# A streaming-encoder block: the mixer's values as one wide block, and its scaled queries in tiles of their own

## The chip, the cores and the metric

One core of a Trainium2 chip runs the whole program. The metric is the device time of one execution in microseconds (us), and the number of a kernel is the median of its runs. For explaining, one execution is recorded by the hardware profiler; its span runs from the first to the last instruction.

The engines are TensorE (PE: matrix products into PSUM; PEld is its loading of weights), VectorE (DVE), ScalarE (ACT), GpSimd (POOL) and SyncE (SP, which issues the DMAs here). Each takes its instructions in order; semaphores make one wait for another.

## What is computed

256 frames of 2048 features go through one layer: a feed-forward half-step, a mixer, an attention over 256 memory tokens, a second feed-forward half-step. All is float32. The change lies in the mixer. Cut to what matters, with its four heads and chunks of 64 frames:

```python
h = rms_norm(x, mix_norm)
u, q, k, v, g, a_lr = split(h @ w_in)          # 1024, 512, 512, 1024, 1024, 16 columns
y_pool = pool_mixer(u, pool_w, pool_scale)     # 4 groups: trailing means - token, then a 256x256 map
# gated linear attention, per head (dk 128, dv 256), chunk-causal:
log_a  = log_sigmoid(a_lr @ w_a2 + b_a) / 16;  cum = cumsum(log_a) in the chunk
k_dec  = k * exp(b_end - cum)                  # b_end: cum at the end of the chunk
scores = q_scaled . k_dec                      # q_scaled has the decay of the chunks between
o      = scores @ v;  o = rms_norm(o) * head_norm * silu(g)
x = x + concat(y_pool, o) @ w_out
```

## The kernel before, in words

**Units of weights.** All large products are made of units of one MB of weights (128 x 2048 floats in SBUF). A unit is loaded by SP into `raw` (three buffers), split into a rounded high part (`wh`, ACT) and a rest (`wl`, DVE), three buffers each, and then used by PE: high by high, high by rest, rest by high, three products for each 128-row step and half of the frames. `Stream.emit` writes the program out: ahead of a unit's products it puts the split of the unit two further on, and behind each split the load of the unit three further on. `st.op(f, n)` puts a piece of work behind the n-th unit from there. The chain `in_turn` keeps the splits in order on ACT and DVE; all the rest may be set between by the framework's planner, which fixes each engine's order at compile time by its own estimate of the times. So an engine's order need not be that of the program.

**Three forms of a block.** `block_a` (weights stationary, the frames streaming) gives the result transposed and holds two PSUM tiles `pa`. `block_b` (frames stationary) makes 512 columns out of four units of 24 products and holds one PSUM tile `pb`. `block_s` (`block_t` without sevens is its plain form) makes 1024 columns out of eight units. For a pair of 128-row steps for which sums of the frames' blocks were computed ahead (`Sums`, here `qk_sums` for the pairs 1 and 3, kept in `ys` 12 to 15), its unit is a "seven": seven block products in place of eight, 21 instructions in place of 24. A seven's weights are summed first on DVE (`T`, L486), and then two sets are split: `xh`, `xl` (one buffer each in the mixer) and `wh`, `wl`. Its PSUM is two tiles for whole results from the first unit on and two more for parts from the first seven on; behind the last seven `combine` adds up the parts (L574 to L579), and behind the last unit `join` adds both (L589).

**PSUM** has four tiles of two banks each (`ptile`), for everything.

**The mixer's order.** First queries and keys (one `block_s` of 1024 columns, with `qk_sums`), then the decay (`load_a`, `decay`), then the pool's columns (two `block_a`, groups 0 and 1, then 2 and 3), the values (two `block_b` of 512 columns, written to `v` by `ev_v`, L1137), with the pool's own product (`pool_unit`, L1027) between these two, then the gate (two `block_a`), then `w_out`. Around the values:
- `ev_pool` (L986) turns a pool group's product into its means: a chain of DVE steps (L319, L323, L997, L1001, L1005) in three `m4` tiles, of which there are three in all, and a split into `ys` 8 + 2g.
- `scores(h)` (L1142) copies and scales the queries (L1150 on ACT, L1152 on DVE) into another `m4` tile, multiplies with the keys (L1160, PSUM tile `pq`) and copies the result to `ST` (L1166). The four stand behind 0, 2, 4 and 6 units counted from the start of the values.
- `pool_out(g)` scales and splits the pool's product from PSUM (`pp`) into `ys` 2g and 2g + 1 (L236 on ACT, L240 on DVE).
- `attend(h)` (L1168) multiplies scores and values (PSUM tile `po`) and squares and copies the result (L1182 on ACT, L1184 on DVE); `head_norms` and `head_scale` normalise the heads, `ev_g` applies the gate.

Of the kernel before, what the change touches and what calls it, by code (L numbers as in the profile page):

```python
# [7 lines left out]
F32 = mybir.dt.float32  # L8
F32R = mybir.dt.float32r
AF = mybir.ActivationFunctionType  # L10
# [12 lines left out]
H = 4  # L23
# [76 lines left out]
def build(ctx, tc, I, out):  # L100
# [187 lines left out]
    def split_pair(dst, kt, src):  # L288
        split(dst[:, kt : kt + 2, 0, :], dst[:, kt : kt + 2, 1, :], src)
# [315 lines left out]
    def block_b(srcs, act, evict, delay=0):  # L605

        n_k = 4 * len(srcs)
        held = {}

        def unit(gi):  # L610
            def fn(wh, wl):
                if gi == 0:
                    held["ps"] = ptile(uid("pb"))
                wh, wl = (w.rearrange("p (k n) -> p k n", n=NB) for w in (wh, wl))
                for kk in range(4):
                    k = 4 * gi + kk
                    for h in range(2):
                        products(held["ps"][:, h, :], act, k, h, wh[:, kk], wl[:, kk],
                                 k == 0, k == n_k - 1)
            return fn  # L620

        for gi, src in enumerate(srcs):
            st.unit(src, unit(gi))
        st.op(lambda: evict(held["ps"]), delay)
# [6 lines left out]
    def wblock(w, n0, k0=0, nk=KT):  # L631

        def src(k):
            return lambda raw: wload(raw.rearrange("p (k n) -> p k n", n=NB), w, k, 4, n0)
        return [src(k0 + k) for k in range(0, nk, 4)]
# [311 lines left out]
    ffn(I["ffn1_w_gate"][0], I["ffn1_w_up"][0], I["ffn1_w_down"][0], down_first,  # L947
        amid_first)
    st.op(close_scope, 1)
    MIX_HOMES = {"T": [("v", D, 1)], "xh": [("xh", 3 * NB, 1)], "xl": [("xl", 3 * NB, 1)]}  # L950
    st.op(open_scope("s_mix", MIX_HOMES), 1)


# [3 lines left out]
    def mt(name, shape, tag=None, bufs=1):  # L957
        t = whole_lines(scope["pool"], shape, F32, tag or name, uid(name), bufs)
        mix[name] = t
        return t  # L960

    def mixer_constants():
        keep = mt("keep", [P, S])
        nc.gpsimd.memset(keep, 1.0)
        for c in range(S // CH):
            nc.gpsimd.memset(keep[:, c * CH : c * CH + 1], 0.0)
        wa2 = mt("wa2", [32, H * DK])
        for i in range(2):
            nc.sync.dma_start(wa2[16 * i : 16 * i + 16, :], I["gla_w_a2"][0])
        for h in range(H):  # L970
            s = mix["ST", h] = mt("ST", [P, 2, S], bufs=H)
            nc.gpsimd.memset(s[64:128, 0, 0:CH], 0.0)
            nc.gpsimd.memset(s[64:128, 1, 2 * CH : 3 * CH], 0.0)

    st.op(mixer_constants, 2)

    def m4():
        return scope["pool"].tile([P, 2 * 2 * (S + PAD)], F32, tag="m4", name=uid("m4"), bufs=3)
# [3 lines left out]

    def as_four(t):
        return t[:, : 4 * S].rearrange("p (a b) -> p a b", a=4)

    def ev_pool(b):  # L986
        def evict(p, ps):
            g = 2 * b + p
            w = WINDOWS[g]
            u, s0, s1 = (as_pad(m4()) for _ in range(3))  # L990
            L = S + PAD
            nc.gpsimd.memset(u[:, :, :PAD], 0.0)
            joined(ps, u[:, :, PAD:], rows["R"])
            src, dst, other, n = u, s0, s1, 1
            while n < w:
                lo = 2 * n - 1
                nc.vector.tensor_tensor(  # L997
                    out=dst[:, :, lo:L], in0=src[:, :, lo:L], in1=src[:, :, lo - n : L - n], op=ALU.add
                )
                src, dst, other, n = dst, other, dst, 2 * n  # L1000
            nc.vector.scalar_tensor_tensor(  # L1001
                out=src[:, :, PAD : PAD + w - 1], in0=src[:, :, PAD : PAD + w - 1], scalar=float(w),
                in1=bc(invc[:, : w - 1]), op0=ALU.mult, op1=ALU.mult,
            )
            nc.vector.scalar_tensor_tensor(  # L1005
                out=src[:, :, PAD:], in0=src[:, :, PAD:], scalar=1.0 / w, in1=u[:, :, PAD:],
                op0=ALU.mult, op1=ALU.subtract,
            )
            split_pair(ys, 8 + 2 * g, src[:, :, PAD:])
        return evict  # L1010

    def load_pool(raw):
# [5 lines left out]
    def pool_unit(wh, wl):  # L1018
        wh, wl = (w.rearrange("p (g t d) -> p g t d", g=4, t=2) for w in (wh, wl))
        for g in range(4):  # L1020
            if g % 2 == 0:
                two = ptile(uid("pp"))
            ps = two[:, g % 2, :].rearrange("p (a b) -> p a b", a=2)
            for dt in range(2):
                parts = [(w, ct, a) for ct in range(2) for w, a in ((wh, 0), (wl, 0), (wh, 1))]
                for n, (w, ct, a) in enumerate(parts):
                    nc.tensor.matmul(  # L1027
                        ps[:, dt, :], w[:, g, ct, dt * P : (dt + 1) * P],
                        ys[:, 8 + 2 * g + ct, a, :], start=n == 0, stop=n == 5,
                    )  # L1030
            mix["pp", g] = ps

    def pool_out(g):
        for dt in range(2):
            split_scaled(ys, 2 * g + dt, mix["pp", g][:, dt, :], gcol(G_PS + 2 * g + dt))
# [93 lines left out]
    block_a(wblock(w_in, 0), xs, ev_pool(0))  # L1129
    block_a(wblock(w_in, NB), xs, ev_pool(1))  # L1130

    def ev_v(b):
        def evict(ps):
            if b == 0:
                mt("v", [P, 2, 2 * NB])
            for h in range(2):
                nc.scalar.activation(  # L1137
                    mix["v"][:, h, b * NB : (b + 1) * NB], ps[:, h, :], AF.Copy, scale=Rcol[:, h : h + 1]
                )
        return evict  # L1140

    def scores(h):  # L1142
        q, kd, E, F = mix["q"][:, h, :], mix["k"][:, h, :], mix["E"], mix["F"]
        e = lambda c: E[:, 4 * h + c : 4 * h + c + 1]
        f = lambda i: F[:, i, h : h + 1]
        QD = m4()
        at = (0, 3 * CH, 5 * CH)
        factors = {(0, 1): e(1), (0, 2): f(0), (0, 3): f(2), (1, 2): e(2), (1, 3): f(1), (2, 3): e(3)}
        for j in range(3):
            nc.scalar.copy(QD[:, at[j] + j * CH : at[j] + (j + 1) * CH], q[:, j * CH : (j + 1) * CH])  # L1150
            for c in range(j + 1, 4):
                nc.vector.tensor_scalar_mul(  # L1152
                    QD[:, at[j] + c * CH : at[j] + (c + 1) * CH], q[:, c * CH : (c + 1) * CH],
                    factors[j, c],
                )
        ps = ptile(uid("pq"))
        for j in range(4):
            part = slice((j % 2) * CH, (j % 2 + 1) * CH)
            rhs = QD[:, at[j] + j * CH : at[j] + S] if j < 3 else q[:, 3 * CH :]
            nc.tensor.matmul(  # L1160
                ps[part, j // 2, j * CH : S], kd[:, j * CH : (j + 1) * CH], rhs, start=True, stop=True
            )
        s = mix["ST", h]
        for j in range(4):
            part = slice((j % 2) * CH, (j % 2 + 1) * CH)
            nc.vector.tensor_copy(s[part, j // 2, j * CH :], ps[part, j // 2, j * CH : S])  # L1166

    def attend(h):  # L1168
        s, v = mix["ST", h], mix["v"]
        po = ptile(uid("po"))  # L1170
        for vt in range(2):
            col = h * DV + vt * P
            nc.tensor.matmul(  # L1173
                po[:, vt, :S], v[:, 0, col : col + P], s[:, 0, :], start=True, stop=False
            )
            nc.tensor.matmul(
                po[:, vt, 2 * CH : S], v[:, 1, col : col + P], s[:, 1, 2 * CH :], start=False, stop=True
            )
        if h % 2 == 0:
            mix["oz", h // 2] = as_four(m4())  # L1180
        q = mix["osq", h] = ttile()
        nc.scalar.activation(q, po[:, :, :S], AF.Square)  # L1182
        i = h % 2
        nc.vector.tensor_copy(mix["oz", h // 2][:, 2 * i : 2 * i + 2, :], po[:, :, :S])  # L1184
# [37 lines left out]
            split_pair(ys, 8 + 2 * h, t)  # L1222
        return evict

    for h, after in enumerate((0, 2, 4, 6)):
        st.op(lambda h=h: scores(h), after)
    for b in range(2):
        block_b(wblock(w_in, (4 + b) * NB), xs, ev_v(b))
        if b == 0:
            st.unit(load_pool, pool_unit)  # L1230
            for g in range(4):
                st.op(lambda g=g: pool_out(g))
        for i in range(2):
            h = 2 * b + i
            at = 1 + i - b
            st.op(lambda h=h: attend(h), at + 1)
            st.op(lambda h=h: head_squares(h), at + 1)
        st.op(lambda b=b: head_norms(b), 5 - 2 * b)
        st.op(lambda b=b: head_scale(b), 6 - b)
    block_a(wblock(w_in, 6 * NB), xs, ev_g(0), (0, 0))  # L1240
    block_a(wblock(w_in, 7 * NB), xs, ev_g(1))
    st.op(close_scope, 1)
# [401 lines left out]
```

## Time and profile before

| what | value |
|---|---|
| median of 3 runs | 2090.24 us (2089.54 to 2092.51) |
| profiled execution, its own time | 2089.89 us |
| its span, first to last instruction | 2088.1 us |
| DMA moved | 435.94 MB, mean 209 GB/s |
| values products L362 `pb` | 192 (128 + 64), 0.39 us each by themselves |
| stage of the values, 812 to 871 us | PE busy 59.00 us, DVE 38.23, ACT 23.40 |

How to read it: the page gives busy time by engine, the span in 40 slices, the DMA queues, the chain of work that ended last, and the costliest groups of instructions by line. Products of PE overlap, so the time from one to the next is less than the duration of one. In a list of waits a row says who waited for whom, for how long in all, how often, and the longest. In a table of windows a row has the window, its length, busy time and number of instructions of PE, PEld, DVE, ACT and POOL, the granted clock of PE, the DMA share and GB/s. In the chain and the timeline a row begins with its start and its length in us.

### The profile page before, as it was taken

Reading aid. Unit: us, or ns where it says so; the run is one execution under the profiler, and the core shown is the slowest. Engines: PE = TensorE matmul, PEld = TensorE weight load, DVE = VectorE, ACT = ScalarE, POOL = GpSimd, SP = SyncE. Lnnn points to the kernel's source line nnn. Section 1 sums busy time; section 2 is a strip of 40 time slices with the busy share of each in tenths; the row PEclk is TensorE's granted clock in tenths of the full one; section 3 lists DMA queues with packets and bytes.
Section 4 is the critical chain, followed back from the end, with each engine's and each line's share of the span. In section 5 each row is a group of like instructions: output and inputs, shape, how many; then the busy total and the mean of one; then the engine's idle time right before and its main releaser. Section 6 shows DMA issues by size and latency. Waiting matters only on the chain.

```text
span 2088.1 us, 24282 instructions
## 1 busy us (share of the span) xinstructions
PE 2069.6 (99%) x9591; PEld 1724.6 (83%) x9591; DVE 1822.2 (87%) x1727; ACT 1152.4 (55%) x1151; POOL 100.1 (5%) x94
## 2 busy tenths in 40 slices
PE   9999999999999998999999999999999999999998
PEld 7888888888888887888888888888888888888886
DVE  7998899989998758579888887889988999889987
ACT  7655455645554664455756544566554556545554
POOL 0000000000000000000001000000100010000001
PEclk9999999999999999999999999999999999999999
DMA  7666666567666655557855555666576765676664
GB/s 263 204 200 225 237 222 220 183 222 243 222 200 223 230 176 161 162 173 231 270 193 172 172 184 178 205 204 229 188 233 205 242 208 196 225 236 227 206 227 152
DMA packets 129131, 435.94 MB, mean 209 GB/s; under 512 B 9845, under 2 KB 13529, under 8 KB 128633
## 3 DMA queue, kind: packets, MB, share of 16 engines
q1 hardware_dynamic: 128840, 433.86, 62.5%
q8 instruction: 75, 1.23, 0.2%
q10 hardware_dynamic: 176, 0.53, 0.1%
q14 instruction: 40, 0.32, 0.0%
HBM read 417.58 MB, written 16.78 MB: 208 GB/s over the span
## 4 chain that ended last, share of the span: by engine, by line
PE 98%; DVE 1%; DMA 0%; ACT 0%; issue 0%; SPq 0%; DVEq 0%; ACTq 0%
PE pt L362 59%; PE pt L507 28%; PE pa L347 4%; PE pb L362 2%; PE ph L780 1%; PE pl L1338 1%; PE pv L1375 1%; PE px L791 1%; DMA x<-in_x 0%; PE pp L1027 0%; PE pe L362 0%; DVE wl L453 0%; PE pq L1160 0%; PE pa L1054 0%; PE po L1173 0%; PE tm L1285 0%
## 5 line engine op out<-in xcount | busy, mean ns | idle before, releaser
L362 PE MATMUL pt<-wh,xs 128*128 128x512 f32 x2176 | 699.3, 391 | 0.0
L453 DVE TENSOR_TENSOR wl<-raw,wh 128x2048 fp32r<-128x2048 f32 (+1 forms) x249 | 534.0, 2152 | 117.0 <-ACT wh L1602 116.7
L1602 ACT CAST wh<-raw 128x2048 fp32r<-128x2048 f32 x249 | 475.4, 1912 | 263.3 <-PE pt L362 113.4
L362 PEld LDWEIGHTS pt<-wh,xs 128*128 128x128 f32 x2176 | 408.2, 188 | 83.7 <-ACT wh L1602 0.2
L489 ACT CAST wh<-T 128x1024 fp32r<-128x1024 f32 x250 | 262.5, 1054 | 376.1 <-DVE T L486 366.7
L362 PE MATMUL pt<-wh,ys 128*128 128x512 f32 x1440 | 455.1, 390 | 0.0
L362 PE MATMUL pt<-wl,xs 128*128 128x512 f32 x1088 | 424.8, 391 | 0.0
L362 PEld LDWEIGHTS pt<-wh,ys 128*128 128x128 f32 x1440 | 270.3, 188 | 55.6
L453 DVE TENSOR_TENSOR wl<-T,wh 128x2048 fp32r<-128x2048 f32 (+1 forms) x125 | 280.7, 2246 | 2.5 <-ACT wh L489 2.2
L362 PE MATMUL pt<-wl,ys 128*128 128x512 f32 x720 | 281.1, 391 | 0.0
L362 PEld LDWEIGHTS pt<-wl,xs 128*128 128x128 f32 x1088 | 204.6, 188 | 41.5
L280 DVE TENSOR_TENSOR xl<-raw,xh 128x1536 fp32r<-128x1536 f32 x125 | 218.9, 1751 | 13.6 <-ACT xh L279 13.5
L279 ACT CAST xh<-raw 128x1536 fp32r<-128x1536 f32 x125 | 185.0, 1480 | 59.1 <-PE pt L507 36.6
L486 DVE TENSOR_TENSOR T<-T,raw 128x512 f32<-128x512 f32 x250 | 172.5, 690 | 6.5
L362 PEld LDWEIGHTS pt<-wl,ys 128*128 128x128 f32 x720 | 135.2, 188 | 28.2 <-DVE wl L453 0.3
L486 DVE TENSOR_TENSOR T<-raw 128x1024 f32<-128x1024 f32 x125 | 152.3, 1218 | 0.5
L507 PE MATMUL pt<-wh,xs 128*128 128x512 f32 x380 | 147.9, 390 | 0.0
L457 POOL TENSOR_TENSOR wl<-raw,wh 128x768 fp32r<-128x768 f32 x42 | 78.0, 1857 | 1453.7 <-DVE wl L453 1444.6
L507 PE MATMUL pt<-xh,xs 128*128 128x512 f32 x384 | 143.4, 390 | 0.0
L507 PE MATMUL pt<-wh,xe 128*128 128x512 f32 x320 | 124.5, 389 | 0.0
L347 PE MATMUL pa<-xs,wh 128*128 128x512 f32 x256 | 90.7, 399 | 0.0
L507 PEld LDWEIGHTS pt<-xh,xs 128*128 128x128 f32 x384 | 72.1, 188 | 14.9
(256 smaller groups left out, 2360.0 us busy)
## 6 DMA issues: line engine op xcount, KB each, us to landing
raw<-in_ffn_w_down SPq DMA_DIRECT2D x88, 1024.0 KB, 5.5
raw<-in_ffn_w_up SPq DMA_DIRECT2D x80, 1024.0 KB, 5.0
raw<-in_ffn_w_gate SPq DMA_DIRECT2D x77, 1024.0 KB, 5.1
raw<-in_w_in SPq DMA_DIRECT2D x32, 1024.0 KB, 5.2
raw<-in_xattn_w_kv SPq DMA_DIRECT2D x32, 1024.0 KB, 5.1
raw<-in_w_out SPq DMA_DIRECT2D x16, 1024.0 KB, 5.6
raw<-in_xattn_w_q SPq DMA_DIRECT2D x16, 1024.0 KB, 5.5
raw<-in_xattn_w_o SPq DMA_DIRECT2D x16, 1024.0 KB, 5.5
```

The lines of the kernel that those rows point to most:

```text
L279: in_turn("scalar", lambda: nc.scalar.copy(hi, src))
L280: in_turn("vector", lambda: nc.vector.tensor_tensor(out=lo, in0=src, in1=f32(hi), op=ALU.subtract))
L347: nc.tensor.matmul(o, w, x, start=k == 0 and i == 0, stop=last and i == 1)
L362: nc.tensor.matmul(ps, a, w, start=first and i == 0, stop=last and i == 2)
L453: in_turn("vector", lambda: nc.vector.tensor_tensor(out=lo[:, :n], in0=src[:, :n], in1=f32(hi[:, :n]), op=ALU.subtract))
L457: rest = nc.gpsimd.tensor_tensor(out=lo[:, n:], in0=src[:, n:], in1=f32(hi[:, n:]), op=ALU.subtract)
L486: in_turn("vector", lambda: nc.vector.tensor_tensor(out=o, in0=a, in1=b, op=ALU.add))
L489: in_turn("scalar", lambda: nc.scalar.copy(th[:, c], t[:, c]))
L507: nc.tensor.matmul(banks[n], x, w, start=n in fresh and j == 0, stop=n in ends and j == 2)
L780: nc.tensor.transpose(v[:, i, h * P : (h + 1) * P], g[:, h, i * P : (i + 1) * P], ident)
L791: nc.tensor.transpose(v[:, j, h * P : (h + 1) * P], x[:, h, j * P : (j + 1) * P], ident)
L1602: in_turn("scalar", lambda: nc.scalar.copy(hi, raw))
```

## The change

The scaled queries leave the `m4` tiles: those of even heads go to the tile `xh`, those of odd heads to `xl`, which the sevens of the mixer use too. The weights' sums `T` of the sevens get a tile of their own, no longer shared with `v`. The score tiles `ST` are no longer four tiles of their own, zeroed at the mixer's start, but take the tile of `wa2` (even heads) or a `c` tile (odd heads), zeroed when the scores are made. The values are one `block_s` of 1024 columns with the pairs 1 and 3 as sevens, by the factors `qk_sums`; since these must stay in `ys` 12 to 15, the pooled values of groups 2 and 3 go to `ys` 0 and 2. Scores 0 and 1 stand behind the first and the second unit of the values; the pool's product comes behind all eight; then `attend` 0, and one gate unit further on each, scores 2 and `attend` 1, scores 3 and `attend` 2, `attend` 3, with the head norms behind two and four gate units.

```diff
-    MIX_HOMES = {"T": [("v", D, 1)], "xh": [("xh", 3 * NB, 1)], "xl": [("xl", 3 * NB, 1)]}
+    MIX_HOMES = {"T": [("T", D, 1)], "xh": [("xh", 3 * NB, 1)], "xl": [("xl", 3 * NB, 1)]}
...
-        for h in range(H):
-            s = mix["ST", h] = mt("ST", [P, 2, S], bufs=H)
-            nc.gpsimd.memset(s[64:128, 0, 0:CH], 0.0)
-            nc.gpsimd.memset(s[64:128, 1, 2 * CH : 3 * CH], 0.0)
...
+    POOLED = (8, 10, 0, 2)
...
-            split_pair(ys, 8 + 2 * g, src[:, :, PAD:])
+            split_pair(ys, POOLED[g], src[:, :, PAD:])
...
-                        ys[:, 8 + 2 * g + ct, a, :], start=n == 0, stop=n == 5,
+                        ys[:, POOLED[g] + ct, a, :], start=n == 0, stop=n == 5,
...
-    def ev_v(b):
-        def evict(ps):
-            if b == 0:
-                mt("v", [P, 2, 2 * NB])
-            for h in range(2):
-                nc.scalar.activation(
-                    mix["v"][:, h, b * NB : (b + 1) * NB], ps[:, h, :], AF.Copy, scale=Rcol[:, h : h + 1]
-                )
-        return evict
+    def v_home():
+        return mt("v", [P, 4, NB])
+
+    def ev_v(j, c):
+        for h in range(2):
+            nc.scalar.activation(c[:, h, :], c[:, h, :], AF.Copy, scale=Rcol[:, h : h + 1])
+
+    def v_part(t, col):
+        j, at = divmod(col, NB)
+        return mix["v"][:, 2 * (1 - j) + t, at : at + P]
+
+    def score_tile(h):
+        s = mix["ST", h] = ctile() if h % 2 else mt("ST", [P, 2, S], "wa2")
+        nc.gpsimd.memset(s[64:128, 0, 0:CH], 0.0)
+        nc.gpsimd.memset(s[64:128, 1, 2 * CH : 3 * CH], 0.0)
+        return s
...
-        QD = m4()
+        QD = scope["pool"].tile([P, 3 * NB], F32, tag=("xh", "xl")[h % 2], name=uid("QD"), bufs=1)
...
-        s = mix["ST", h]
+        s = score_tile(h)
...
-    for h, after in enumerate((0, 2, 4, 6)):
-        st.op(lambda h=h: scores(h), after)
-    for b in range(2):
-        block_b(wblock(w_in, (4 + b) * NB), xs, ev_v(b))
-        if b == 0:
-            st.unit(load_pool, pool_unit)
-            for g in range(4):
-                st.op(lambda g=g: pool_out(g))
-        for i in range(2):
-            h = 2 * b + i
-            at = 1 + i - b
-            st.op(lambda h=h: attend(h), at + 1)
-            st.op(lambda h=h: head_squares(h), at + 1)
-        st.op(lambda b=b: head_norms(b), 5 - 2 * b)
-        st.op(lambda b=b: head_scale(b), 6 - b)
+    for h in range(2):
+        st.op(lambda h=h: scores(h), 1 + h)
+    block_s(wwide(w_in, 4 * NB), xs, qk_sums, (0, 2, 4, 5, 1, 6, 3, 7), ev_v, home=v_home)
+    st.unit(load_pool, pool_unit)
+    for g in range(4):
+        st.op(lambda g=g: pool_out(g))
+    for h in range(2):
+        st.op(lambda h=h: attend(h), h)
+        st.op(lambda h=h: head_squares(h), h)
+        st.op(lambda h=h: scores(2 + h), h + 1)
+        st.op(lambda h=h: attend(2 + h), h + 2)
+        st.op(lambda h=h: head_squares(2 + h), h + 2)
+    for b in range(2):
+        st.op(lambda b=b: head_norms(b), 2 + 2 * b)
+        st.op(lambda b=b: head_scale(b), 3 + 2 * b)
```

In `attend` the values are read as `v_part(t, col)` in place of `v[:, t, col : col + P]`.

More of the change, by code (lines that the diff above doesn't have):

```diff
@@ L1168, in attend @@
     def attend(h):
-        s, v = mix["ST", h], mix["v"]
+        s = mix["ST", h]
         po = ptile(uid("po"))
@@ L1173, in attend @@
             nc.tensor.matmul(
-                po[:, vt, :S], v[:, 0, col : col + P], s[:, 0, :], start=True, stop=False
+                po[:, vt, :S], v_part(0, col), s[:, 0, :], start=True, stop=False
             )
             nc.tensor.matmul(
-                po[:, vt, 2 * CH : S], v[:, 1, col : col + P], s[:, 1, 2 * CH :], start=False, stop=True
+                po[:, vt, 2 * CH : S], v_part(1, col), s[:, 1, 2 * CH :], start=False, stop=True
             )
```

## The prediction

> **What bounds the kernel now.** I read the page first: the busy shares, then the chain that ended last.
>
> ```profile
> span 2088.1 us, 24282 instructions
> PE 2069.6 (99%) x9591; PEld 1724.6 (83%) x9591; DVE 1822.2 (87%) x1727; ACT 1152.4 (55%) x1151; POOL 100.1 (5%) x94
> PE 98%; DVE 1%; DMA 0%; ACT 0%; issue 0%; SPq 0%; DVEq 0%; ACTq 0%
> ```
>
> TensorE (PE) bounds nearly everything: only two things shorten this kernel, fewer products, or the 18.5 us (2088.1 - 2069.6) in which PE has nothing. So next come PE's waits, whole span, then the chain around the only long one.
>
> ```profile
> PE pq L1160 <- DVE m L1152: 6.6, 1, 6.6
> ...
> PE pt L507 <- DVE xl L280: 0.2, 1, 0.2
> ```
>
> ```profile
> 804.88 0.70 DVE m L319
> ...
> 807.04 2.29 DVE wl L453
> 809.32 0.64 DVE m L997
> ...
> 810.91 0.50 DVE m L1152 x3
> ...
> 811.54 1.08 PE pq L1160 x2
> 812.63 5.99 PE pb L362 x18
> ...
> 827.82 0.57 PE pq L1160 x2
> ```
>
> The reader should see that PE's largest wait sits exactly where the change works. PE's queue is in order, and head 0's score products (`pq`) stand ahead of the first values product. They wait for scaled queries (L1152), which live in an `m4` tile; the three `m4` tiles are in the hands of pool group 2, so DVE must finish its sums (L319 to L997) first, with a weight split (L453) among them. Then the clock:
>
> ```profile
> 804.00:808.00 4.00, 0.91 (x5) 0.51 (x4) 3.74 (x5) 2.97 (x3) 0.00 (x0) 1.00 0.46 134
> 808.00:811.00 3.00, 0.00 (x0) 0.00 (x0) 2.93 (x6) 0.21 (x2) 0.00 (x0) 0.73 0.64 196
> 811.00:816.00 5.00, 4.46 (x10) 3.06 (x11) 4.01 (x11) 0.95 (x4) 0.12 (x1) 0.50 0.53 195
> 816.00:818.00 2.00, 2.00 (x9) 1.58 (x9) 0.00 (x0) 0.00 (x0) 0.00 (x0) 0.95 0.00 0
> ```
>
> The third number from the end is the granted clock: full for the first 3 us of the wait, 0.50 from 811 to 816, back by 818. The wait costs more than itself.
>
> **The change, part by part.** The stages' products, again from the chain:
>
> ```profile
> 636.83 14.31 PE pt L362 x63
> ...
> 770.83 33.40 PE pa L347 x188
> ...
> 831.93 6.79 PE pb L362 x29
> ...
> 839.52 5.95 PE pp L1027 x48
> 845.47 5.47 PE pb L362 x24
> ...
> 857.40 0.43 PE po L1173 x2
> ...
> 858.71 5.49 PE pb L362 x24
> ```
>
> 1. Seven products for two pairs. A values unit has 24 products in 5.47 us, 0.228 us each (a product's own 0.39 us overlaps the next). Two of eight units now have 21: 6 x 0.228 = **-1.4 us**. The factors they need (`qk_sums`) are already there for the query and key block, so nothing is computed anew; keeping them in `ys` 12 to 15 is what moves the pooled values to `ys` 8, 10, 0, 2, at no cost in instructions.
>
> 2. The wait for the queries. Head 0's scores come after the first values unit (5.5 us later) and their tile is the weight split's `xh`, free here, as the sevens come later. **-6.6 us.** What is late next? PE goes straight to values unit 0. Weights are split two units ahead, so the split L453 at 807.04, ended at 809.3, is unit 2's, and units 0 and 1 are ready; it is needed at 804.9 + 2 x 5.5 + 0.8 of scores = 816.7. Nothing is late. If the scaling were done only at 810.9 to 812.4, as now, PE would wait some 2 us at 810.4, less than the 3 us for which the clock stayed full above; that is inside the range.
>
> 3. The clock. Its 2 score products took 1.08 us, later 0.57: 0.51. The 18 values products took 5.99; at 6.79 / 29 = 0.234 they take 4.21: 1.78. **-2.3 us.** The Trainium skill, "TensorE: Matmul & The Clock Gate", section "What's actually happening", says that an idle window of about 3.4 us halves the clock and 3.4 us of work restores it. By that rule the loss would be an estimated 1.7 us, and the sum 0.6 us smaller; the halving agrees with the 0.50 here, and the loss I take from the rows.
>
> 4. DVE's load. A seven costs four kinds of row in place of one split; behind the sevens come the sums of parts:
>
> ```profile
> L453 DVE TENSOR_TENSOR wl<-T,wh 128x2048 fp32r<-128x2048 f32 (+1 forms) x125 | 280.7, 2246 | 2.5 <-ACT wh L489 2.2
> L280 DVE TENSOR_TENSOR xl<-raw,xh 128x1536 fp32r<-128x1536 f32 x125 | 218.9, 1751 | 13.6 <-ACT xh L279 13.5
> L486 DVE TENSOR_TENSOR T<-T,raw 128x512 f32<-128x512 f32 x250 | 172.5, 690 | 6.5
> L486 DVE TENSOR_TENSOR T<-raw 128x1024 f32<-128x1024 f32 x125 | 152.3, 1218 | 0.5
> L589 DVE TENSOR_TENSOR sg<-pt,sg 128x1024 f32<-128x1024 f32 x52 | 62.2, 1217 | 5.8 <-PE pt L362 5.7
> 100.00:150.00 50.00, 50.00 (x230) 41.63 (x229) 49.60 (x40) 31.33 (x27) 1.86 (x1) 1.00 0.61 203
> 812.00:871.00 59.00, 59.00 (x289) 47.69 (x288) 38.23 (x67) 23.40 (x31) 0.12 (x1) 0.96 0.45 141
> ```
>
> Per seven 2.25 + 1.75 + 2 x 0.69 + 1.22 = 6.6 us on DVE against 2.2: +4.4, twice 8.8. Combining adds 1.22 + 2 x 0.69 = 2.6, the two joins 2.4. That is 14 us more; the stage had 59.00 - 38.23 = 21 us of DVE idle, and two heads' scores leave it. The last row but one shows the cover: DVE busy 49.60 of 50 us and PE without a gap. **0 us**; if the cover is gone, each seven is late by 6.6 - 21 x 0.227 (14.31 / 63) = 1.8 us, together 3.7. ACT has more room (23.40 of 59).
>
> 5. PSUM. There are four tiles; the wide block holds two from its first unit and all four from its first seven until its parts are combined; a narrow block held one. Scores of heads 0 and 1 meet two free tiles: nothing. Behind the block stand the pool products (two tiles, those of the parts), head 0's `po` and the gate's `pa` (two at once). The fifth of these has to wait for pool group 1's output, and this hand-over is slow:
>
> ```profile
> 844.70 0.48 ACT L236 ACTIVATE ys<-pp,gains 128x256 fp32r<-128x256 f32 x1 [1.60 <-DVE ys L240]
> ...
> 847.68 0.84 ACT L236 ACTIVATE ys<-pp,gains 128x256 fp32r<-128x256 f32 x2
> 850.02 0.87 DVE L240 SCALAR_TENSOR_TENSOR ys<-pp,gains,ys 128x256 fp32r<-128x256 f32 x2
> ```
>
> ACT and DVE take turns on a bank (ACT waits 1.60 for DVE), with weight splits between, and group 1 is done at 850.5, 5.0 us after the last pool product at 845.47. Moreover `ys` 0 to 3 now hold what the pool products of groups 2 and 3 read, so groups 0 and 1 cannot be written before those end. PE has head 0's `po` to do (857.40 to 858.71, 1.3 us) and four gate products (4 x 33.40 / 188 = 0.7): the wait is 5.0 - 2.0 = 3.0 at most. At best the turns take 4 x 0.48 = 1.9 us, and it is nothing. I take the middle, **+1.6 us**. The skill's page "PSUM — Partial Sum Buffer", section "PSUM bank collisions raise a hardware error", forbids two engines in one bank at a time, which fits these turns and speaks against the change; the price is from the rows.
>
> 6. Priced at nothing: `T` in a tile of its own only removes a wait for the values tile; the eight zeroings move along on POOL (5% busy); the score tiles in `wa2` and `c` are free by then; the loads carry the same bytes in wider rows, with SP's order kept; scaling the values moves no instruction (four before and after), and their last is ready some 4 to 5 us after the block (two joins of 1.2, two pairs of scalings of 1.3), with 5.95 us of pool products as cover; without it 1 to 2 us of wait at head 0's `po`.
>
> Sum: -1.4 - 6.6 - 2.3 + 1.6 = -8.7. The profiled execution took 2089.89 us (span 2088.1 and 1.8 around it), so 2081.2; the median of the runs is 0.35 above it: **2081.5 us**.
>
> **The rivals.**
> A. No new wait: -10.3, 2079.9. For it: once started, PE waits nowhere else by over 0.2 us in the whole trace. Against it: five claims on four tiles occur in none that I found.
> B. The wait only moves, the change not doing what it says of the queries. In the order of the program pool group 3 comes ahead of head 0's scores. If DVE keeps that order, its chain (eight steps of 0.7 us, like L319 above, and a short one: 5.8 us, from when group 2 lets go after L1005, at 812.0 to 812.4) ends at 818 to 819; PE stands at the scores from 810.4, waits some 8 and loses the clock's 2.3 again: -10.3 + 10.3 = 0, 2090.2. Against it, from DVE's timeline:
>
> ```profile
> 810.83 0.25 DVE L1152 TENSOR_SCALAR m<-q,E 128x64 f32<-128x64 f32 x1
> ...
> 811.31 0.68 DVE L1005 SCALAR_TENSOR_TENSOR m<-m,m 128x512 f32<-128x512 f32 x1
> ```
>
> Head 0's scaling (L1152) stands ahead of group 2's own last step (L1005), which the program has earlier: the queue does not follow the program's order.
> C. Slower, by PSUM behind the values block. Scores 2 and 3, `po` 1 to 3, two head norms and a head scale, eight users, now share the two tiles that `pa` leaves, in its first four units; before, heads 0 to 3's scores and two `po` stood in the values block, with three free. Now a `po` tile is let go late:
>
> ```profile
> 861.63 0.68 DVE L1184 COPY m<-po 128x512 f32<-128x512 f32 x1
> ```
>
> Its products ended at 858.7, so 3.6 us. If each user waits out the one before, 8 x 3.6 = 29, less the 2 x 5.6 us that a second tile hides: +18, 2098. It decides from 10.3 / 8 = 1.3 us of wait for each user, and shows as over 0.2% from 1.8. Against it: gate products on `pa` can go between.
>
> **How the numbers follow.** Forecast (new waits between 0.5 and 6 us: 2080.4 to 2086) 0.56; A 0.15; B 0.17; C 0.12. Since 0.2% (4.2 us) is about what a measurement of this kernel can tell, faster means below 2086.1: forecast, A and a sliver of B, 0.72. Same: most of B, 0.16. Slower: C, 0.12. The range leaves out C and the edge of A: 2079.0 to 2090.5.
>
> **What would show it.** Right: PE's wait list without `pq`; the clock at 1.00 through the stage; 186 values products (21 in two units) under `pt`, none under `pb`; any new wait at the gate's first `pa` or at `po`, released by ACT or DVE. Wrong: `pq` still in PE's waits (B); `pa` or `po` waiting several times behind the pool (C); a seven waiting for `xl` or `wl` from DVE (item 4 mispriced); or any wait over 3 us, which brings 2.3 more.

## The result and the profile after

The changed kernel takes 2078.3 us (median of 6 runs, 2077.68 to 2079.33), the kernel before 2090.22 (median of 6, 2088.17 to 2092.51): a ratio of 0.9943, 95% interval 0.993 to 0.9956, or 11.9 us less. The forecast was 2081.5, with a range from 2079.0 to 2090.5: the direction was right, the gain of 8.7 us too small, and the result lies 0.7 us below the range. The profiled execution took 2078.49 us, 11.4 less than the one before.

PE's waits over the whole span of the changed kernel, longest first:

```profile
PE pwarm L206 <- POOL ident masks.py:199: 1.4, 1, 1.4
PE px L717 <- DMA x<-in_x: 1.3, 1, 1.3
PE pt L362 <- ACT xs L236: 0.4, 1, 0.4
PE pt L507 <- DVE xl L280: 0.2, 1, 0.2
PE pt L362 <- DVE wl L453: 0.2, 1, 0.2
```

The row `pq` with its 6.6 us is gone, and no new wait in the mixer has taken its place: the first three rows lie in the first 60 us, the last two behind 912. The same stretches as in the prediction, with the granted clock third from the end, and then the whole time of the values:

```profile
804.00:808.00 4.00, 4.00 (x20) 3.31 (x19) 3.86 (x6) 2.95 (x3) 0.23 (x2) 1.00 0.70 225
808.00:811.00 3.00, 3.00 (x19) 2.18 (x18) 2.41 (x4) 0.82 (x1) 0.13 (x1) 1.00 0.38 87
811.00:816.00 5.00, 5.00 (x23) 4.11 (x24) 4.91 (x9) 3.09 (x3) 0.23 (x2) 1.00 0.48 188
804.00:850.00 46.00, 46.00 (x217) 37.62 (x216) 43.87 (x59) 22.78 (x24) 2.75 (x7) 1.00 0.56 183
```

The clock stays full, and PE is busy for all of 46 us although DVE is busy for 43.87 of them. The chain that ended last is PE alone from the pool's columns to `w_out`:

```profile
770.55 34.08 PE pa L347 x192
804.63 5.46 PE pt L362 x24
810.09 0.79 PE pq L1165 x6
810.89 5.67 PE pt L362 x24
816.56 0.80 PE pq L1165 x6
817.36 11.11 PE pt L362 x48
828.47 4.76 PE pt L507 x21
...
848.87 5.75 PE pp L1025 x48
854.62 0.43 PE po L1178 x2
855.05 1.73 PE pa L347 x10
...
857.66 9.54 PE pa L347 x54
867.20 0.79 PE pq L1165 x6
...
910.27 19.76 PE pt L362 x87
```

What to read off: a score is now one piece of 0.79 us (before, heads 0 and 1 came in two pieces each, 1.08 + 0.58 and 0.57 + 0.59); a seven takes 4.76 us where a plain unit takes 5.46; and behind the pool's product 64 gate products follow with only the rest of `po` between them. (The last row is only as long as the view, which ended at 930 us.)

One number serves to compare all kernels: the **stage**, from the start of the long run of 192 products of the pool's columns, behind the decay's eight `pz` products, to the first product of `w_out`. (In the kernel before, the chain holds 188 of the 192.) Before it is 921.96 - 770.83 = 151.13 us, after 910.27 - 770.55 = 139.72. The 11.41 us between them are all that the spans of the two profiled executions differ by (2088.1 - 2076.7 = 11.4).

### The profile page after: what moved, and what is told of

The parts are those of the page before. It is cut to its first block, busy times and chain, and to the rows that moved or that the text cites. A ratio compares the mean times of both kernels' runs of the same rounds, so it can differ in the third digit from the quotient of the medians.

```text
span 2076.7 us, 24301 instructions
## 1 busy us (share of the span) xinstructions
PE 2064.0 (99%) x9585; PEld 1720.6 (83%) x9585; DVE 1833.9 (88%) x1740; ACT 1158.5 (56%) x1158; POOL 103.8 (5%) x96
## 4 chain that ended last, share of the span: by engine, by line
PE 99%; DVE 0%; ACT 0%; DMA 0%; issue 0%; SPq 0%; DVEq 0%; ACTq 0%
PE pt L362 61%; PE pt L507 29%; PE pa L347 4%; PE ph L780 1%; PE pl L1343 1%; PE pv L1380 1%; PE px L791 0%; DMA x<-in_x 0%; PE pp L1025 0%; PE pe L362 0%; DVE wl L453 0%; PE po L1178 0%; PE pa L1052 0%; PE tm L1290 0%; PE px L717 0%; PE pq L1165 0%
## 5 line engine op out<-in xcount | busy, mean ns | idle before, releaser
L362 PE MATMUL pt<-wh,xs 128*128 128x512 f32 x2272 | 729.2, 390 | 0.4 <-ACT xs L236 0.4
L453 DVE TENSOR_TENSOR wl<-raw,wh 128x2048 fp32r<-128x2048 f32 (+1 forms) x247 | 527.6, 2143 | 95.0 <-ACT wh L1607 94.7
L362 PEld LDWEIGHTS pt<-wh,xs 128*128 128x128 f32 x2272 | 425.8, 188 | 88.2 <-ACT xs L236 0.7
L489 ACT CAST wh<-T 128x1024 fp32r<-128x1024 f32 x254 | 266.8, 1054 | 383.9 <-DVE T L486 374.3
L362 PE MATMUL pt<-wl,xs 128*128 128x512 f32 x1136 | 442.9, 390 | 0.0
L453 DVE TENSOR_TENSOR wl<-T,wh 128x2048 fp32r<-128x2048 f32 (+1 forms) x127 | 285.2, 2246 | 2.5 <-ACT wh L489 2.2
L362 PEld LDWEIGHTS pt<-wl,xs 128*128 128x128 f32 x1136 | 213.4, 188 | 43.4 <-DVE wl L280 0.2
L507 PE MATMUL pt<-wh,xs 128*128 128x512 f32 x384 | 149.2, 389 | 0.0
```

The lines of the kernel that those rows point to most:

```text
L362: nc.tensor.matmul(ps, a, w, start=first and i == 0, stop=last and i == 2)
L453: in_turn("vector", lambda: nc.vector.tensor_tensor(out=lo[:, :n], in0=src[:, :n], in1=f32(hi[:, :n]), op=ALU.subtract))
L489: in_turn("scalar", lambda: nc.scalar.copy(th[:, c], t[:, c]))
L507: nc.tensor.matmul(banks[n], x, w, start=n in fresh and j == 0, stop=n in ends and j == 2)
```

## Experiments

Theory: the wait comes from the `m4` tile in which the queries stood, it costs itself and the clock, and the seven products are worth their 1.4 us. Rivals: the later place of the scores does it; or the sevens cost as much elsewhere as they bring. The stage is read from each kernel's own chain (for e8 its start from PE's timeline), from one profiled execution each; the last column is the difference from the kernel that the row varies.

| kernel | runs' median, us | before, beside it | stage, us | difference |
|---|---|---|---|---|
| before | | | 151.13 | |
| e1_tile_only | 2079.31 | 2089.49 | 141.13 | -10.00 (before) |
| e2_place_only | 2081.23 | 2089.49 | 142.99 | -8.14 (before) |
| changed | 2078.3 | 2090.22 | 139.72 | -11.41 (before) |
| e3_m4_again | 2080.59 | 2089.49 | 142.14 | +2.42 (changed) |
| e4_place_again | 2077.9 | 2089.49 | 139.69 | -0.03 (changed) |
| e5_no_sevens | 2079.24 | 2089.25 | 140.92 | +1.20 (changed) |
| e6_split_scores | 2078.23 | 2089.25 | 140.35 | +0.63 (changed) |
| e7_gate_in_order | 2084.28 | 2089.25 | 146.76 | +7.04 (changed) |
| e8_third_seven | 2077.99 | 2089.76 | 139.72 | 0.00 (changed) |
| e9_changed_again | 2078.45 | 2089.76 | 139.72 | 0.00 (changed) |

The changed kernel's second profiled execution (e9) repeats the stage to 0.01 us. That is one repeat only, but it lets differences of some tenths in the stage be read even where the medians can't tell them.

**The tile alone, in the kernel before (e1)**

```diff
-        QD = m4()
+        QD = scope["pool"].tile([P, 3 * NB], F32, tag=("xh", "xl")[h % 2], name=uid("QD"), bufs=1)
```

> The kernel before, with the scaled queries in xh and xl and nothing else of the change. Theory: PE waited because head 0's queries stood in an m4 tile behind pool group 2; so the tile alone removes the wait of 6.6 us and the clock's 2.3, and the scores of heads 0 and 1 are no longer cut in two (1.1 us more): 2090.2 - 10.0 = 2080.2, with no pq in PE's waits by over 0.5 us. Rival (the place): the scores still stand ahead of the first values unit, and the scaling still queues on DVE behind pool group 2, so a wait of 4 us or more at pq remains and the time is 2086 to 2090.

Measured: 2079.31 (ratio 0.9952, 0.9937 to 0.9967). DVE's timeline of this kernel shows where the scaling went:

```profile
785.50 1.07 DVE L1152 TENSOR_SCALAR QD<-q,E 128x64 f32<-128x64 f32 x6
...
787.15 0.74 DVE L1152 TENSOR_SCALAR QD<-q,F 128x64 f32<-128x64 f32 x4
...
790.61 0.42 DVE L1152 TENSOR_SCALAR QD<-q,F 128x64 f32<-128x64 f32 x2
```

All twelve scalings of heads 0 and 1 run at 785 to 791, as soon as the decay is known and 14 us before PE wants them; in the kernel before, the first ran at 810.83. PE's chain has the first `pq` right behind the pool's columns, in one piece:

```profile
805.02 0.80 PE pq L1160 x6
```

The stage is 10.00 us shorter; the wait is 6.63 of that in the timeline and the clock 2.29 by the rows of the prediction, so 1.08 is left, which the theory gave to the scores that are no longer cut in two (1.1). The rival (4 us or more of wait left) falls.

**The place alone, in the kernel before (e2)**

```diff
-    for h, after in enumerate((0, 2, 4, 6)):
+    for h, after in enumerate((1, 2, 4, 6)):
```

> The kernel before, with head 0's scores one values unit later (behind 1, 2, 4 and 6 units in place of 0, 2, 4 and 6), the queries still in m4 tiles. Theory (the tile): the queries now wait for pool group 3 as well; either PE waits some 8 us at pq and loses the clock's 2.3 again (2090), or the planner, which sees the tile taken, puts the scores further back, and the wait goes for that reason alone (2080 to 2082). Rival (the place): one unit later is enough by itself, head 0's scores stand right behind the first unit with no wait, 2080.

Measured: 2081.23 (0.9963, 0.9949 to 0.9977). From PE's waits, the chain and the windows of this kernel:

```profile
PE pq L1160 <- ACT m L1150: 1.8, 1, 1.8
```

```profile
826.18 0.68 ACT v L1137
826.86 1.79 ACT wh L1602
828.65 0.15 ACT m L1150
828.80 0.04 issue
828.84 0.65 PE pq L1160 x2
829.49 2.21 PE pp L1027 x17
831.70 0.58 PE pq L1160 x5
```

```profile
826.00:829.00 3.00, 1.16 (x15) 0.81 (x12) 2.51 (x11) 3.00 (x7) 0.00 (x0) 1.00 0.92 319
829.00:834.00 5.00, 5.00 (x40) 4.37 (x40) 4.87 (x12) 0.99 (x5) 0.00 (x0) 1.00 0.04 11
```

The planner did not put head 0's scores behind one unit but behind four. That it did so because it saw the tile taken is inferred: with the tile of their own (e1, e4) the scores stand where the program has them. Behind the four units they wait for ACT, which scales the values and casts a weight first, and one score is again cut in two. The wait of 1.8 us leaves the clock at 1.00. So the place alone takes away most, 8.1 us of the stage, but by pushing the scores back and not by the one unit.

**The changed kernel with the queries back in `m4` (e3)** (only the line of the first experiment undone)

> The changed kernel with the scaled queries back in m4 tiles, all else as changed. By the prediction's rival B: wait of 8 us at pq and 2.3 of clock, 2088.6. By what the changed kernel's order of products suggests (the planner puts products that it sees ready in front of those whose tile is taken): the scores of heads 0 and 1 move back to between the fifth and the sixth values unit, no wait over 0.5 us, and the time stays within 2 us of the changed kernel's 2078.3.

Measured: 2080.59 (0.9957, 0.9942 to 0.9972), 2.3 us above the changed kernel, a little more than the 2 us expected, with no wait at `pq`. As in the kernel with the place alone, the scores moved back, to behind five units and between the two sevens (833 to 836 us), and the stage is 2.42 us longer. The wait of rival B in the prediction does not come, because here the planner does not leave such a score in front; the tile is still worth 2.4 us. In the kernel before, the planner did leave it in front and PE stood 6.6 us; why there and not here, no run shows. PE's named waits there hold only 0.6 of them (0.35 for `xl`, 0.21 for a score copy); the rest, in small gaps around the second seven and the head norms, I did not take apart.

**The changed kernel with the old place (e4)**

```diff
-        st.op(lambda h=h: scores(h), 1 + h)
+        st.op(lambda h=h: scores(h), 2 * h)
```

> The changed kernel with the scores of heads 0 and 1 behind 0 and 2 values units again (in place of 1 and 2), queries in their own tiles. Theory (the tile): the queries can be scaled ahead of pool group 2's sums, so PE waits under 0.5 us at the first pq: 2078 to 2079. Rival (the place): PE reaches the first scores 5.5 us earlier than in the changed kernel and waits 2 us or more there, 2080 to 2087.

Measured: 2077.9 (0.9945, 0.9931 to 0.996), stage -0.03. With the tile, the place is worth nothing; the rival falls.

**The changed kernel without sevens (e5)**

```diff
-    block_s(wwide(w_in, 4 * NB), xs, qk_sums, (0, 2, 4, 5, 1, 6, 3, 7), ev_v, home=v_home)
+    block_t(wwide(w_in, 4 * NB), xs, ev_v)
```

`ev_v` then scales from PSUM into `v`.

> The changed kernel with the values as a plain wide block: 24 products in each of the eight units, no sevens, no parts to combine. Theory: a product costs 0.227 us wherever it stands, so the stage is 6 x 0.227 = 1.4 us longer and nothing else changes: 2079.7. Rival (the sevens cost something on the way: DVE's load, the four PSUM tiles, the changed order of the gate's products): without them the time is the same or shorter, 2077 to 2078.5.

Measured: 2079.24 (0.9952, 0.9939 to 0.9964), stage +1.20; the first experiment to the changed kernel gives 1.41 the other way round. The products are worth 6 x 0.227 = 1.36 by the rows, and the two differences lie within 0.2 of it; the medians (0.9 apart) agree in sign, no more.

**The changed kernel with the scores of heads 0 and 1 in two pieces (e6)**

```diff
+        if h > 1:
+            score_products(h, range(4))
+            score_copies(h)
+        else:
+            score_products(h, (0,))
...
+        st.op(lambda h=h: score_products(h, (1, 2, 3)), 2 + h)
+        st.op(lambda h=h: score_copies(h), 2 + h)
```

> The changed kernel with the score products of heads 0 and 1 cut in two: the first of the four behind one unit, the other three one unit later, each at a unit's end. Theory: a change between 512-column products and score products costs PE about 0.2 us on the way out and some more on the way in, so a score cut in two costs 0.4 to 0.6 more; head 1's first piece joins head 0's second, so there are three changes in place of two: 2078.3 + 0.5 = 2078.8, and the stage from the first values product to the first of w_out is 0.3 to 0.7 us longer. Rival: the products cost the same in any place and order, and the stage's length stays within 0.1 us.

Measured: 2078.23 (0.9947, 0.9935 to 0.996), which the runs can't tell from 2078.3; the stage is 0.63 us longer, as the theory had it. Its chain through the values begins so:

```profile
803.80 5.46 PE pt L362 x24
809.27 0.58 PE pq L1174 x2
809.84 5.67 PE pt L362 x24
815.51 0.80 PE pq L1174 x6
816.32 5.71 PE pt L362 x24
822.02 0.58 PE pq L1174 x5
```

There are pieces of 0.58, 0.80 and 0.58 us where the changed kernel has 0.79 and 0.80, which is 0.4, and one stretch of values more that begins behind a score: 24 products take 5.67 us there and 5.46 elsewhere, 0.2 more. This is the price of one further change. The kernel before has two, as each score is cut by itself. By its rows, with the first piece at its full-clock 0.57, the pieces 0.57 + 0.58 and 0.57 + 0.59 are 0.7 more than the two whole scores of 0.80 in e1, and two more stretches behind a score add 0.4: that is the 1.08 that e1 left over.

**The changed kernel with the first gate block in the program's order (e7)**

```diff
+                            if strict and "before" in held:
+                                with tc.issue_after(held["before"].ins):
+                                    held["before"] = product()
...
-    block_a(wblock(w_in, 6 * NB), xs, ev_g(0), (0, 0))
+    block_a(wblock(w_in, 6 * NB), xs, ev_g(0), (0, 0), strict=True)
```

> The changed kernel with the products of the first gate block bound to the program's order (column groups 0 to 3 for each 128-row step), so that the planner can't run the groups 0 and 1 of three units ahead of groups 2 and 3. Theory: the hand-over of PSUM from the pool's product is as slow as the prediction took it (5 us), and only the planner's order hides it; bound to the program's order PE waits 2 to 4 us for the second pa tile: 2080.3 to 2082.3 (over 3.4 us of wait the clock would add up to 2.3). Rival: the second tile is free in time, no wait, 2078.3.

Measured: 2084.28 (0.9975, 0.9966 to 0.9984), so 6 us of the gain are lost. PE's wait, its chain and the windows of this kernel (its line numbers are 1 higher at `pa` and 6 higher behind it):

```profile
PE pa L348 <- DVE m L1195: 4.1, 1, 4.1
```

```profile
854.49 1.90 ACT wh L1613
856.38 0.02 issue
856.41 2.29 DVE wl L459
858.70 0.79 DVE ys L240 x2
859.49 0.61 DVE m L1195
860.10 0.04 issue
860.14 7.94 PE pa L348 x28
```

```profile
856.00:860.00 4.00, 0.08 (x1) 0.00 (x0) 3.59 (x4) 2.47 (x6) 0.23 (x2) 0.93 0.63 230
860.00:862.00 2.00, 1.86 (x5) 1.60 (x6) 1.85 (x6) 0.86 (x2) 0.00 (x0) 0.50 0.90 261
862.00:865.00 3.00, 3.00 (x11) 2.59 (x10) 0.23 (x1) 0.00 (x0) 0.00 (x0) 0.50 0.43 165
865.00:868.00 3.00, 3.00 (x14) 2.38 (x13) 0.00 (x0) 0.00 (x0) 0.00 (x0) 0.79 0.00 0
```

Here is the hand-over that the prediction feared: a weight split on ACT and on DVE, output of the pool (L240), head 0's copy (L1195), and only then a second tile. PE stands 4.1 us, just above the 2 to 4 expected, the clock falls to 0.50, and the stage is 7.04 us longer: 4.1 of wait and 2.7 of clock (see the last section) make 6.8 of it. In the changed kernel the same steps end just as late:

```profile
859.16 0.87 DVE L240 SCALAR_TENSOR_TENSOR ys<-pp,gains,ys 128x256 fp32r<-128x256 f32 x2
859.95 0.68 DVE L1189 COPY m<-po 128x512 f32<-128x512 f32 x1
```

yet PE doesn't wait, because its order there is another. The trace does not say which of the two `pa` tiles a product writes, but the next weight split does. It needs the buffer of the first gate unit, which the program's order would let go with the unit's 32nd product, at 857.66 + 22 x 0.177 = 861.6. In the changed kernel it starts behind all 64:

```profile
867.17 1.90 ACT L1607 CAST wh<-raw 128x2048 fp32r<-128x2048 f32 x1 [4.91 <-PE pa L347]
```

This fits an order with 48 products of the first tile, 16 from each of three weight units, ahead of the 16 that the first unit has for the second tile, which so is wanted at 857.66 + 38 x 0.177 = 864.4 only.

**A third seven in the values block (e8), and the changed kernel again (e9)**

```diff
-    qk_sums = Sums("qe", xs, (1, 3), False, 2, {0: in_ys(6), 1: in_ys(7)})
+    qk_sums = Sums("qe", xs, (1, 3, 5), False, 3, {0: in_ys(6), 1: in_ys(7), 2: in_ys(3)})
...
-    block_s(wwide(w_in, 4 * NB), xs, qk_sums, (0, 2, 4, 5, 1, 6, 3, 7), ev_v, home=v_home)
+    block_s(wwide(w_in, 4 * NB), xs, qk_sums, (0, 2, 1, 4, 3, 6, 5, 7), ev_v, home=v_home)
```

The queries and keys keep two sevens; the pair 5's factors are made during the pool's columns, and scores 0 and 1 stand ahead of the block.

> The changed kernel with a third seven in the values block (the pair 5 too; its factors are computed on DVE during the pool's columns, into ys 6 and 7, which are free until the pool's output), and the scores of heads 0 and 1 ahead of the block, so that the sevens may start earlier. It tests where the cover for DVE's load ends: the changed kernel has DVE busy 43.87 of 46 us from 804 to 850 with no wait of PE. Theory: 3 x 0.227 = 0.7 us of products go, but 4.4 us more of DVE work no longer fits in the stage, so PE waits 1 to 4 us for weights (xl or wl): 2078.6 to 2081.6. Rival: DVE's other work in the stage moves aside, no wait over 0.3 us: 2077.6.

> The changed kernel itself, beside the kernel with a third seven on the same chip: 2078.3 as before, the stage from the pool's first product to the first of w_out 139.7 us, with a spread of some 0.2 us from one profiled execution to the next.

Measured: 2077.99 (0.9945, 0.9931 to 0.9958) and 2078.45 (0.9948, 0.9935 to 0.996), not to be told apart; the two stages are equal. The repeat of the changed kernel is 11.3 us faster than the kernel before beside it. Both expectations for the third seven missed: three products fewer save 0.7 us, and two small waits, 0.9 together, give it back. Two rows of PE's waits and the window of the values:

```profile
PE po L1179 <- ACT v L1136: 0.5, 1, 0.5
PE pt L362 <- DVE m L319: 0.4, 1, 0.4
```

```profile
804.00:850.00 46.00, 45.64 (x218) 37.72 (x217) 45.65 (x62) 24.28 (x26) 2.21 (x4) 1.00 0.52 167
```

DVE is busy 45.65 of 46 us, so the cover of the prediction's item 4 is used up here. But neither wait is for a seven's weights (`xl` or `wl`), the price that item 4 and the theory named: one ends with a step of the pool's means (L319), the other with the scaling of the values on ACT. This run also moved the scores and the sevens' order, and other arrangements of a third seven were not run.

## Why the prediction came out too small

- **The bound, and the wait as the thing to win (items 2 and 3): right.** 6.6 us for the wait and 2.3 for the clock, with the 1.1 below, are what e1's stage holds, and L1152 moved to where nothing is in its way. Of the two means named in item 2, the later place and the tile, the tile is what counts; beside it the place adds nothing (e4), though alone it takes away 8.1 us (e2).
- **Seven products for two pairs, -1.4: right.** 1.41 from e1 to the changed kernel, 1.20 from e5. As the first of these holds all the rest of the change too, the items priced at nothing (item 6) come to about nothing together.
- **DVE's load at nothing (item 4): right**, and close to its end: with DVE busy 43.87 of 46 us no wait shows, with 45.65 of 46 two small ones do (e8).
- **The term that was left out: -1.1.** The prediction's own row (`pq` in pieces of 1.08 and 0.58, with 18 values products between) showed the score cut in two. I used its first piece for the clock and did not ask what the cut itself costs. It costs about 0.6 us for a cut (e6), twice in the kernel before, and with their queries ready early the scores are in one piece.
- **The step that failed: item 5, "I take the middle, +1.6 us", measured as 0.** The lateness of the hand-over was right, even too small: nothing is free before some 860 us, and bound to the program's order it costs 4.1 us of wait and with the clock 7.0 (e7), where I put 3.0 at most. By the profile the tile that PE then gets is let go by head 0's copy, one step behind the pool's output that item 5 names. What I missed is that the planner, at compile time, may order PE's products around a missing tile. I allowed for the four products that the program has there; the changed kernel's order has, by the reading above, 48. The same holds for rival C ("gate products on `pa` can go between") and for rival B, where the planner moved the scores rather than let PE stand (e2, e3).
- So rival A (no new wait) was the case to forecast: -10.3, with the left-out 1.1 it is -11.4. That this is the stage's 11.41 proves little, as 1.08 and 1.41 are themselves differences of stages; with e5's 1.20 and twice e6's 0.63 in their place it is 11.4 too. The two errors bring the forecast from 2081.5 to 2078.8. The 0.5 us left to the measured 2078.3 is no more than the medians of the kernel before differ by from one set of runs to the next (2089.25 to 2090.22). Rival A's chance of 0.15 looks too low: my reason against it, five claims on four tiles, counted claims and not what PE has to do meanwhile. The range's lower end was set 0.9 us below A with nothing left for a term not seen; had only one of the two terms been wrong, the result would have lain inside.

## What to carry to other kernels

A tile that is free at the right time may be worth more than a later place in the program: a buffer shared with a long chain holds back work whose inputs have been ready for 20 us, and the wait is then put down to the engine that does the work. Where a planner orders the instructions, price a missing buffer by the work that it may bring forward, not only by what the program has next, and look whether it did: in the kernel before it let PE stand. And where a small product is cut in two by large ones, count the changes, about 0.6 us for each cut here.

## What the runs showed of the hardware

Three waits of PE with what the clock did: 1.8 us (e2) left it at 1.00; 4.1 us (e7) and 6.6 us (before) halved it. It fell 3.4 us after PE's last product in e7 and 4.5 us in the kernel before, reckoned from the windows with a mean of 0.93 (856 to 860) and 0.73 (808 to 811). Once PE was at work again it stayed halved from 860.1 to 866.3 and from 811.5 to 816.2, 6.1 and 4.7 us, reckoned from the windows with 0.79 and 0.95. This cost 2.7 us (18 gate products in 5.93 us, which take 18 x 0.177 = 3.2 at full clock) and 2.3 us. The longer wait did not cost more clock than the shorter. The Trainium skill, "TensorE: Matmul & The Clock Gate", section "What's actually happening", has the clock fall after an idle window of about 3.4 us and come back after about 3.4 us of work, in windows that run freely. The first agrees with these three waits; the return took longer here, 4.7 and 6.1 us.
